# The Fourier branch of an encoder block, computed in halves: even and odd in token and channel

## The chip, the cores and the metric

The kernel runs on one core of a Trainium2 chip. A core has a matrix engine (TensorE, PE in the profile; PEld is its loading of stationary tiles), a vector engine (VectorE, DVE), a scalar engine (ScalarE, ACT), a general one (GpSimd, POOL) and a sync engine (SP) from which most transfers from memory are issued. Each engine has a queue of its own and works it off in order; semaphores tie the queues together. The metric is the device time of one execution in microseconds (us); for several runs, their median.

## The reference

One encoder block for 256 tokens (SEQ) of 2048 channels (D_MODEL), in float32. Two token mixers work side by side on the normalised input: a gated DeltaNet with 8 heads of 128 and a Fourier branch with 8 groups of 128 channels. Their outputs are gated channel by channel, added and projected, and a squared-ReLU MLP follows. Cut to what matters here:

```python
h = rms_norm(x, g_mix[l])
q, k, v, z, f, scal, gates = jnp.split(h @ w_in[l], SPLIT_POINTS, axis=-1)
y_a = gated_deltanet_branch(q, k, v, z, scal, ...)     # ends with  ... @ w_dn_up
y_f = fourier_branch(f, w_fourier[l])
gate_a, gate_f = jnp.split(jax.nn.sigmoid(gates), N_BRANCHES, axis=-1)
x = x + (gate_a * y_a + gate_f * y_f) @ w_o[l]

def fourier_branch(f, w_lin):
    fg = f.astype(jnp.float32).reshape(b, t, N_FOURIER_GROUPS, FOURIER_GROUP_DIM)
    fr = jnp.real(jnp.fft.fft2(fg, axes=(1, 3), norm="ortho"))
    return fr.reshape(b, t, FOURIER_WIDTH).astype(f.dtype) @ w_lin
```

For each group the real part of the two-dimensional transform over tokens and channels is C_T f C_D - S_T f S_D, with cosine and sine tables. Cosine is even and sine odd under the reflection of a token t to 256 - t and of a channel d to 128 - d.

## The kernel before

Every product is made in split precision: each operand is cut into a high part and a low part (type fp32r), and high times high, high times low and low times high are added up, three matmuls for one. Activations are cut once. Weights are cut on the fly. A weight tile of 128 x 1024 floats (512 KB) is loaded by SP into one of four buffers named `raw`; `split` makes its high part `hi` on ACT (L88) and its low part `lo` on DVE (L92), three buffers each; TensorE then uses them. `wtiles` hands out the buffers. Two routines use them around the change:

- `stream(src, nk, ahi, alo)` holds the activations stationary (128 tokens of one k tile, for two token halves tb) and moves weights of 512 columns: 6 matmuls for each k (L167 to L169). A chunk of 512 outputs with 16 k tiles is 96 matmuls and 8 weight tiles; with 8 k tiles it is half of that.
- `split` also cuts results that go into the next product, such as `o_hi` and `o_lo`.

The program around the change, in order:

- `dn_group(0)` and `dn_group(1)`: the DeltaNet. Its buffers are in the pool `pd`. Its last part, `dn_out`, forms the heads' outputs `ohat` (L602), their norms and, on POOL, the factors `fsc` (L614). Matmuls of the following gates fill its pauses on TensorE.
- `gates` 0 to 3: four chunks of the DeltaNet gate, `stream` over `w_g` and a tanh on ACT into the columns of `merged`.
- the head norm: `ohat` times `fsc` and `zs` (L671), four transposes for each group and token half (L675), split into `o_hi` and `o_lo`.
- w_dn: `stream` over `w_dn` in four chunks with `o_hi` and `o_lo`; the gate is multiplied in. Then the pool `pd` is closed.
- the f projection: `stream` over the last two chunks of `w_in`, 1024 Fourier channels. `f1`, `fe`: sum and difference of the two token halves (t and t + 128), split into `f_hi`, `f_lo`.
- the DFT: eight groups, each with 6 matmuls along tokens (L722 to L727) and 6 along channels (L736), 256 columns each, then a split into `fr_hi`, `fr_lo`.
- `gates_f` 0 to 3, chunks 4 to 7 of the gates, and after each (one chunk ahead) `merge`: `stream` over `w_fo` with `fr_hi`, `fr_lo`, gate and sum (L752, L753), transposes (L756), split into `m_hi`, `m_lo`.
- `xres` and `gfin`, loaded on ACT's queue into memory that the merge's pool `pf` leaves; then w_o, `stream` over four chunks with `m_hi`, `m_lo`, and the MLP.

The program is written in this order, but a scheduler that works on the whole program places each instruction in its engine's queue, so that queues can differ from the code's order where no dependence forbids it. Pools are memory: a tile that takes the place of another waits until that one's last user is done.

## Time and profile before

| | us |
|---|---|
| median of three runs | 1401.39 (1400.87 to 1401.4) |
| the profiled execution | 1398.59 |
| its span in the trace | 1396.9 |
| TensorE busy in it | 1381.9 |
| VectorE busy in it | 864.6 |
| ScalarE busy in it | 689.5 |
| one low part of a weight tile on VectorE | 1.224 |
| one high part of a weight tile on ScalarE | 1.060 |

The span is the time from the first to the last instruction that the profiler recorded in one execution; durations below are from that execution. Busy time of TensorE is modelled from the starts of pipelined matmuls: the mean duration that a row gives for one matmul is longer than the distance from one start to the next. A row of the timeline gives start and duration in us, the engine, the line, the operation, output and inputs, shapes and count; a row of the groups gives the count, the busy us, the mean ns of one and the idle time of the engine just before. A row of the windows gives a stretch of the span, the busy time and count of each engine in it, the granted clock of TensorE as a share of full speed, the busy share of the transfer engines and GB/s.

### The profile page before, as it was taken

To read this page: it belongs to the slowest core of one execution; us is meant where nothing else is said; L and a number is where in the kernel's file an instruction comes from. 1 tells how busy PE (TensorE), PEld (TensorE's weight loads), DVE (VectorE), ACT (ScalarE), POOL (GpSimd) and SP (SyncE) were. 2 spreads that over 40 slices of the span, in tenths; PEclk is the share of its full clock that TensorE was granted. 3 is DMA by queue.
4 is the path that set the end of the run, shared out by engine and by line. 5 is a ranking of instruction groups with operands and counts; after the bars stand their busy time and mean duration, and the time that the engine had idled before them with its cause. 6 is when DMAs were issued, how large, how long until landed. Compare 5 with 4: busy or idle time off the path is not lost.

```text
span 1396.9 us, 20162 instructions
## 1 busy us (share of the span) xinstructions
PE 1381.9 (99%) x7838; PEld 1195.6 (86%) x7838; DVE 864.6 (62%) x1239; ACT 689.5 (49%) x1042; POOL 35.8 (3%) x60
## 2 busy tenths in 40 slices
PE   9999999999999999999999999999999999999997
PEld 8999997888888888888888888888888888888897
DVE  7869997845556555656666665444456666644553
ACT  6586746545435444445545544333344544444443
POOL 2001100101000000000000000000000000000000
PEclk9999999999999999999999999999999999999999
DMA  8556466354566556676555556666655555666663
GB/s 286 151 169 176 157 162 175 104 151 136 184 204 180 152 181 187 210 251 183 183 192 185 189 185 189 192 194 194 196 188 188 186 191 183 187 193 194 194 195 122
DMA packets 94544, 255.63 MB, mean 183 GB/s; under 512 B 25456, under 2 KB 33648, under 8 KB 94064
## 3 DMA queue, kind: packets, MB, share of 16 engines
q1 hardware_dynamic: 93456, 250.15, 58.4%
q10 hardware_dynamic: 992, 4.19, 0.8%
q8 instruction: 61, 1.00, 0.3%
q14 instruction: 35, 0.29, 0.1%
HBM read 251.16 MB, written 3.15 MB: 182 GB/s over the span
## 4 chain that ended last, share of the span: by engine, by line
PE 95%; issue 1%; DVE 1%; DMA 1%; ACT 1%; SPq 0%; POOLq 0%; POOL 0%; DVEq 0%; ACTq 0%
PE mm L146 17%; PE mm L167 10%; PE mm L168 10%; PE mm L169 10%; PE mm L145 8%; PE mm L829 8%; PE mm L827 8%; PE mm L828 8%; PE mm L122 3%; PE mm L121 3%; PE mm L127 3%; PE mm L148 1%; DMA raw<-in_w_k_dram 0%; PE aux L736 0%; DVE lo L92 0%
## 5 line engine op out<-in xcount | busy, mean ns | idle before, releaser
L92 DVE TENSOR_TENSOR lo<-raw,hi 128x1024 fp32r<-128x1024 f32 (+1 forms) x459 | 560.3, 1221 | 396.1 <-ACT hi L88 390.7
L88 ACT ACTIVATE hi<-raw 128x1024 fp32r<-128x1024 f32 (+1 forms) x459 | 485.6, 1058 | 475.9 <-PE mm L829 185.8
L146 PE MATMUL mm<-hh,hi 128*128 128x512 f32 x1024 | 356.8, 398 | 0.0
L145 PE MATMUL mm<-hh,lo 128*128 128x256 f32 x960 | 269.3, 281 | 0.0
L146 PEld LDWEIGHTS mm<-hh,hi 128*128 128x128 f32 x1024 | 188.1, 188 | 41.6
L828 PE MATMUL mm<-lo,rh 128*128 128x512 f32 (+1 forms) x512 | 192.3, 376 | 0.0
L829 PE MATMUL mm<-hi,rl 128*128 128x512 f32 (+1 forms) x512 | 192.3, 376 | 0.0
L145 PEld LDWEIGHTS mm<-hh,lo 128*128 128x128 f32 x960 | 181.5, 189 | 2.9
L827 PE MATMUL mm<-hi,rh 128*128 128x512 f32 (+1 forms) x512 | 173.7, 376 | 0.0
L168 PE MATMUL mm<-lo,hh 128*128 128x512 f32 x384 | 151.6, 395 | 0.0
L169 PE MATMUL mm<-hi,hh 128*128 128x512 f32 x384 | 150.9, 393 | 0.0
L167 PE MATMUL mm<-hi,hh 128*128 128x512 f32 x384 | 143.2, 394 | 0.4 <-ACT merged L653 0.4
L828 PEld LDWEIGHTS mm<-lo,rh 128*128 128x128 f32 x512 | 96.4, 188 | 17.6
L829 PEld LDWEIGHTS mm<-hi,rl 128*128 128x128 f32 x512 | 96.4, 188 | 17.4
L827 PEld LDWEIGHTS mm<-hi,rh 128*128 128x128 f32 x512 | 96.3, 188 | 17.3
L122 PE MATMUL mm<-hh,hi 128*128 128x256 f32 x320 | 90.6, 283 | 0.0
L121 PE MATMUL mm<-hh,hi 128*128 128x256 f32 x320 | 90.5, 283 | 0.0
L127 PE MATMUL mm<-hh,lo 128*128 128x256 f32 x320 | 90.4, 283 | 0.0
L167 PEld LDWEIGHTS mm<-hi,hh 128*128 128x128 f32 x384 | 72.3, 189 | 15.5 <-ACT merged L653 0.6
L168 PEld LDWEIGHTS mm<-lo,hh 128*128 128x128 f32 x384 | 72.5, 189 | 14.3
L169 PEld LDWEIGHTS mm<-hi,hh 128*128 128x128 f32 x384 | 72.6, 189 | 14.0
L152 ACT COPY rt<-mm 128x256 f32<-128x256 f32 x64 | 23.9, 373 | 109.1 <-PE mm L146 109.1
(312 smaller groups left out, 1654.1 us busy)
## 6 DMA issues: line engine op xcount, KB each, us to landing
raw<-in_w_up_dram SPq DMA_DIRECT2D x128, 512.0 KB, 3.7
raw<-in_w_down_dram SPq DMA_DIRECT2D x128, 512.0 KB, 3.5
raw<-in_w_g_dram SPq DMA_DIRECT2D x64, 512.0 KB, 3.8
raw<-in_w_qkv_dram SPq DMA_DIRECT2D x40, 512.0 KB, 4.3
raw<-in_w_in_dram SPq DMA_DIRECT2D x32, 512.0 KB, 3.9
raw<-in_w_o_dram SPq DMA_DIRECT2D x32, 512.0 KB, 4.3
raw<-in_w_dn_dram SPq DMA_DIRECT2D x16, 512.0 KB, 3.6
raw<-in_w_fo_dram SPq DMA_DIRECT2D x16, 512.0 KB, 3.5
```

The lines of the kernel that those rows point to most:

```text
L88: act.activation(hi, src, AF.Copy, scale=scale)
L92: dve.tensor_tensor(lo, src2, hi.bitcast(F32), op=ALU.subtract)
L121: first = pe.matmul(o, hv[:, cs], ahi[:, k, :], start=(k == 0), stop=False)
L122: pe.matmul(o, hv[:, cs], alo[:, k, :], start=False, stop=False)
L145: pe.matmul(ps[:, 0:T], lv[:, cs], ab[:, k, 0], start=False, stop=False)
L146: pe.matmul(ps, hv[:, cs], ab[:, k].rearrange("p a b -> p (a b)"), start=(k == 0), stop=(k == KD - 1))
L167: pe.matmul(ps[tb], ah, hi[:, kk, :], start=(k == 0), stop=False)
L168: pe.matmul(ps[tb], ah, lo[:, kk, :], start=False, stop=False)
L169: pe.matmul(ps[tb], al, hi[:, kk, :], start=False, stop=(k == nk - 1))
L827: pe.matmul(ps[tb], ah, hi[:, kk, :], start=(k == 0), stop=False)
L828: pe.matmul(ps[tb], ah, lo[:, kk, :], start=False, stop=False)
L829: pe.matmul(ps[tb], al_, hi[:, kk, :], start=False, stop=(k == 31))
```

## The change

The Fourier branch now uses the reflections. Instead of f, the sums and differences of reflected tokens (`ev`: t plus 256 - t, 129 columns padded to 130; `od`: t minus 256 - t, 128 columns) are multiplied with the sums and differences of the weights of reflected channels (d plus 128 - d, and d minus 128 - d). Each pair of 512 KB weight tiles `w_fa`, `w_fb` (channels below 64, and their reflections) is added and subtracted on chip by `halves`, and each result is split like any weight tile. The same is done with `w_fourier` on the output side, in `y_f`. Channel 64 of each group, which is its own reflection, goes apart: `f_last` and the small tables `w_fon`, `dfn`. The tokens are loaded a second time from `xT` and normalised and folded by `fold`. Weights are now stationary and tokens move: `mm2` multiplies a high part with both parts of the tokens (256 or 260 columns) and a low part with the high part (128 or 130 columns), two matmuls where there were three. `f_pair(j)`, for two groups each, gives the even and the odd half of f; `transform` does the DFT on the halves and is placed after the second w_dn chunk; `y_f(n)`, for two times 128 output channels, multiplies with the folded `w_fourier`, joins the halves and leaves channels on the partitions, so that the gates are transposed instead of the result (`channels`).

The order of the stages changes: f_pair and f_last now come ahead of w_dn. The pool `pd` is closed right after the DeltaNet; what lives longer (`ohat`, `zs`, `fsc`, `o_hi`, `o_lo`) moves to a new pool `pk`. The arithmetic of the tables and the reordering of the weights into tiles happen in the preparation of the inputs, with no sums of weights there.

The diff, cut to its core:

```diff
@@ dn_group(1, "q") @@
+    dnp.close()
...
+    def mm2(o, hi, lo, ab, n, start, stop):
+        first = None
+        if not start:
+            first = pe.matmul(o[:, 0:n], lo, ab[:, 0], start=False, stop=False)
+        last = pe.matmul(o, hi, ab.rearrange("p a b -> p (a b)"), start=start, stop=stop)
+        if start:
+            first = last
+            pe.matmul(o[:, 0:n], lo, ab[:, 0], start=False, stop=False)
+        return first, last
...
+    ev = pm.tile([P, KD, 2, E0], F32R, tag="sC", name="ev")
+    od = pm.tile([P, KD, 2, P], F32R, tag="sD", name="od")
+    def fold(c):
+        ks = slice(4 * c, 4 * c + 4)
+        x4 = pq.tile([P, 4, T], F32, tag="x4", bufs=2, name=nm("x4"))
+        nc.sync.dma_start(x4, xT[:, ks, :])
+        for k in range(4):
+            act.activation(x4[:, k, :], x4[:, k, :], AF.Copy, scale=gm[:, 4 * c + k:4 * c + k + 1])
+        dve.tensor_tensor(x4, x4, rbc.unsqueeze(1).to_broadcast([P, 4, T]), op=ALU.mult)
+        e4 = pq.tile([P, 4, E0], F32, tag="e4", bufs=1, name=nm("e4"))
+        o4 = pq.tile([P, 4, P], F32, tag="o4", bufs=1, name=nm("o4"))
+        act.copy(e4[:, :, 0:E0:P], x4[:, :, 0:E0:P])
+        act.activation(e4[:, :, E0 - 1:E0], x4[:, :, 0:1], AF.Copy, scale=0.0)
+        act.activation(o4[:, :, 0:1], x4[:, :, 0:1], AF.Copy, scale=0.0)
+        dve.tensor_tensor(e4[:, :, 1:P], x4[:, :, 1:P], x4[:, :, T - 1:P:-1], op=ALU.add)
+        dve.tensor_tensor(o4[:, :, 1:P], x4[:, :, 1:P], x4[:, :, T - 1:P:-1], op=ALU.subtract)
+        split(ev[:, ks, 0, :], ev[:, ks, 1, :], e4)
+        split(od[:, ks, 0, :], od[:, ks, 1, :], o4)
+    def halves(a_src, b_src):
+        ra, _, _ = wtiles(parts=False)
+        rb, _, _ = wtiles(parts=False)
+        nc.sync.dma_start(ra.rearrange("p a b -> p (a b)"), a_src)
+        nc.sync.dma_start(rb.rearrange("p a b -> p (a b)"), b_src)
+        rp = pf.tile([P, KP, NW], F32, tag="rp", bufs=2, name=nm("rp"))
+        _, ph, pl = wtiles(raw=False)
+        dve.tensor_tensor(rp, ra, rb, op=ALU.add)
+        split(ph, pl, rp)
+        _, mh, ml = wtiles(raw=False)
+        dve.tensor_tensor(ra, ra, rb, op=ALU.subtract)
+        split(mh, ml, ra)
+        return [tuple(x.rearrange("p a b -> p (a b)") for x in t) for t in ((ph, pl), (mh, ml))]
+    def sum_halves(dst, ps, n):
+        act.copy(dst, ps[:, n:2 * n])
+        dve.tensor_tensor(dst, ps[:, 0:n], dst, op=ALU.add)
...
+    def f_pair(j):
+        pp, pq_ = mm_ps()[:, 0:2 * E0], mm_ps()[:, 0:2 * P]
+        for q in range(2):
+            wp, wm = halves(w_fa[j, :, q * 1024:q * 1024 + 1024], w_fb[j, :, q * 1024:q * 1024 + 1024])
+            for (o, w, ab, n) in ((pp, wp, ev, E0), (pq_, wm, od, P)):
+                for kk in range(8):
+                    k = 8 * q + kk
+                    cs = slice(kk * P, kk * P + P)
+                    mm2(o, w[0][:, cs], w[1][:, cs], ab[:, k], n, k == 0, k == KD - 1)
+        es = pf.tile([P, E0], F32, tag="es", bufs=1, name=nm("es"))
+        os_ = pf.tile([P, P], F32, tag="os", bufs=1, name=nm("os"))
+        sum_halves(es, pp, E0)
+        split(Ph[:, j], Pl[:, j], es)
+        sum_halves(os_, pq_, P)
+        split(Qh[:, j], Ql[:, j], os_)
+    def f_last():
+        raw, hi, lo = wtiles(1, P)
+        nc.sync.dma_start(raw[:, 0], w_fn)
+        split(hi, lo, raw)
+        ps = mm_ps()[0:8, 0:2 * E0]
+        for k in range(KD):
+            cs = slice(8 * k, 8 * k + 8)
+            mm2(ps, hi[:, 0, cs], lo[:, 0, cs], ev[:, k], E0, k == 0, k == KD - 1)
+        es = pf.tile([8, E0], F32, tag="es", bufs=1, name=nm("es"))
+        sum_halves(es, ps, E0)
+        split(P8h, P8l, es)
...
+    def y_f(n):
+        wp, wm = halves(w_fo[n // 2, 0], w_fo[n // 2, 1])
+        raw = pt_.tile([8, 256], F32, tag="w8", bufs=1, name=nm("w8"))
+        nc.sync.dma_start(raw, w_fon[:, n * P:n * P + 256])
+        w8 = tuple(pt_.tile([8, 256], F32R, tag=f"w8{i}", bufs=1, name=nm("w8")) for i in range(2))
+        split(w8[0], w8[1], raw)
+        e = pt_.tile([P, 2, E0], F32, tag="ee", bufs=1, name=nm("ee"))
+        oc = pt_.tile([P, 2, P], F32, tag="oc", bufs=1, name=nm("oc"))
+        pod = dn_ps()
+        last = None
+        for i in range(2):
+            o = mm_ps()[:, 0:2 * E0]
+            for j in range(4):
+                cs = slice(i * NW + j * P, i * NW + j * P + P)
+                mm2(o, wp[0][:, cs], wp[1][:, cs], fe[:, j], E0, j == 0, False)
+            mm2(o, w8[0][:, i * P:i * P + P], w8[1][:, i * P:i * P + P], f8, E0, False, True)
+            sum_halves(e[:, i], o, E0)
+        for i in range(2):
+            o = pod[:, i * T:i * T + T]
+            for j in range(4):
+                cs = slice(i * NW + j * P, i * NW + j * P + P)
+                first, end = mm2(o, wm[0][:, cs], wm[1][:, cs], fo[:, j], P, j == 0, j == 3)
+                if j == 0:
+                    after(first, last)
+            last = end
+        pv = pod.rearrange("p (i a b) -> p i a b", i=2, a=2)
+        act.copy(oc, pv[:, :, 1])
+        dve.tensor_tensor(oc, pv[:, :, 0], oc, op=ALU.add)
+        y = pt_.tile([P, 2, T], F32, tag="yf", bufs=2, name=nm("yf"))
+        act.copy(y[:, :, P:P + 1], e[:, :, P:P + 1])
+        dve.tensor_tensor(y[:, :, 0:P], e[:, :, 0:P], oc, op=ALU.add)
+        dve.tensor_tensor(y[:, :, P + 1:T], e[:, :, P - 1:0:-1], oc[:, :, P - 1:0:-1], op=ALU.subtract)
+        return y
...
+    with tc.tile_pool(name="pq", bufs=1) as pq:
+        for c in range(4):
+            gates(m_cols(c), c)
+            fold(c)
+            if c < 2:
+                head_norm(c)
+    dd, dn8 = table(dft, P, 2 * E0 + 256, "d"), table(dfn, 8, 5 * E0, "d8")
+    CD, SD = cut(dd, 0, E0), cut(dd, E0, P)
+    CT, ST = cut(dd, E0 + P, E0), cut(dd, 2 * E0 + P, P)
+    CD64 = [cut(dn8, j * E0, E0, 8) for j in range(4)]
+    CT128 = cut(dn8, 4 * E0, E0, 2)
+    for j in range(4):
+        f_pair(j)
+    f_last()
+    fctx2 = ExitStack()
+    for c in range(4):
+        ps = stream(w_dn[c], NH, o_hi, o_lo)
+        for tb, m in enumerate(m_cols(c)):
+            dve.scalar_tensor_tensor(m, m, 1.0, ps[tb], op0=ALU.add, op1=ALU.mult)
+        if c == 1:
+            transform()
+    fctx2.close()
...
-    f_hi = pf.tile([P, 2, 1024], F32R, tag="f_hi", name="f_hi")
-    f_lo = pf.tile([P, 2, 1024], F32R, tag="f_lo", name="f_lo")
-    for c in range(2):
-        ps = stream(w_in[2 + c], KD, h_hi, h_lo)
...
-    for gr in range(8):
...
     tg = gates_f(0)
     for c in range(4):
         nxt = gates_f(c + 1) if c < 3 else None
-        merge(c, tg)
+        for i in range(2):
+            n = 4 * c + 2 * i
+            y = y_f(n)
+            dve.scalar_tensor_tensor(y, channels(tg, 2 * P * i), 1.0, y, op0=ALU.add, op1=ALU.mult)
+            dve.tensor_tensor(y, channels(merged, n * P), y, op=ALU.add)
+            split(m_hi[:, n:n + 2, :], m_lo[:, n:n + 2, :], y)
         tg = nxt
```

`transform`, left out here, makes 102 such products of tables: 72 with stationary tiles of 128 columns and 30 with 2 or 8, all with 128 or 130 moving columns.

What this does to the queues is seen at three places. The first is DVE's queue where the last gate's weights are split, around the head norm. Before (L671 is the head norm's product, L602 the DeltaNet's last outputs, lo_3999 and its followers are low parts of w_dn tiles):

```order
L92 TENSOR_TENSOR lo_3912<-raw_3910,hi_3911 128x1024
L92 TENSOR_TENSOR lo_3930<-raw_3928,hi_3929 128x1024
L671 SCALAR_TENSOR_TENSOR ohat_3247<-ohat_3247,fsc,zs_3054 128x128 x4
L602 SCALAR_TENSOR_TENSOR ohat_3247<-dn_3335,eab,tmp_3250 128x128 x4
L94 SCALAR_TENSOR_TENSOR o_lo<-aux_3955,gh,o_hi 128x4x128
L94 SCALAR_TENSOR_TENSOR o_lo<-aux_3966,gh,o_hi 128x4x128
L92 TENSOR_TENSOR lo_3999<-raw_3997,hi_3998 128x1024
L671 SCALAR_TENSOR_TENSOR ohat_3247<-ohat_3247,fsc,zs_3054 128x128 x4
L92 TENSOR_TENSOR lo_4017<-raw_4015,hi_4016 128x1024
L92 TENSOR_TENSOR lo_4035<-raw_4033,hi_4034 128x1024
```

After (L882 is the head norm's product; L735 and L738 are the sum and the difference of two weight tiles, `rp` and `raw`; L716 the tokens times `rbc`; L722 and L723 the even and odd sums of tokens; `dl` and `d8l` low parts of tables):

```order
L882 SCALAR_TENSOR_TENSOR ohat_3250<-ohat_3250,fsc,zs_3057 128x128 x4
L735 TENSOR_TENSOR rp_4112<-raw_4108,raw_4109 128x1024
L92 TENSOR_TENSOR dl<-raw_4094,dh 128x516
L92 TENSOR_TENSOR d8l<-raw_4100,d8h 8x650
L738 TENSOR_TENSOR raw_4108<-raw_4108,raw_4109 128x1024
L92 TENSOR_TENSOR lo_4114<-rp_4112,hi_4113 128x1024
L716 TENSOR_TENSOR x_423_3529<-x_423_3529,rbc 128x1024
L735 TENSOR_TENSOR rp_4159<-raw_4155,raw_4156 128x1024
L722 TENSOR_TENSOR e_424_3536<-x_423_3529 128x4x127
L723 TENSOR_TENSOR o_425_3537<-x_423_3529 128x4x127
L716 TENSOR_TENSOR x_456_3719<-x_456_3719,rbc 128x1024
L738 TENSOR_TENSOR raw_4155<-raw_4155,raw_4156 128x1024
```

and a few rows on, up to what the first matmul of f_pair needs (`ev`):

```order
L94 SCALAR_TENSOR_TENSOR o_lo_3756<-aux_3741,gh,o_hi_3755 128x4x128
L94 SCALAR_TENSOR_TENSOR o_lo_3756<-aux_3750,gh,o_hi_3755 128x4x128
L92 TENSOR_TENSOR lo_4119<-raw_4108,hi_4118 128x1024
L92 TENSOR_TENSOR lo_4161<-rp_4159,hi_4160 128x1024
L92 TENSOR_TENSOR ev<-e_424_3536,ev 128x4x130
L92 TENSOR_TENSOR od<-o_425_3537,od 128x4x128
```

The low parts of w_dn's tiles, which stood right behind the head norm, have given their place to the folding of tokens and weights.

The second is TensorE's queue at the end of the last gate chunk (mm_3800 and mm_3801 before, mm_3927 and mm_3928 after). Before, transposes of `ohat` and w_dn follow:

```order
L168 MATMUL mm_3801<-lo_3930,hh 128x512
L169 MATMUL mm_3801<-hi_3929,hh 128x512
L675 MATMUL aux_3977<-tr,ohat_3247 128x128 x4
L167 MATMUL mm_3995<-hi_3998,o_hi 128x512
L167 MATMUL mm_3996<-hi_3998,o_hi 128x512
L168 MATMUL mm_3995<-lo_3999,o_hi 128x512
L169 MATMUL mm_3995<-hi_3998,o_lo 128x512
```

After, f_pair's first half follows, with ev and then od:

```order
L171 MATMUL mm_3928<-lo_4057,hh 128x512
L172 MATMUL mm_3928<-hi_4056,hh 128x512
L886 MATMUL aux_3750<-tr,ohat_3250 128x128 x4
L687 MATMUL mm_4106<-ev,hi_4113 128x260
L690 MATMUL mm_4106<-ev,lo_4114 128x130
L686 MATMUL mm_4106<-ev,lo_4114 128x130
...
L687 MATMUL mm_4106<-ev,hi_4113 128x260
L687 MATMUL mm_4107<-od,hi_4118 128x256
L690 MATMUL mm_4107<-od,lo_4119 128x128
L686 MATMUL mm_4107<-od,lo_4119 128x128
```

The matmuls of w_dn now stand behind all of f_pair and f_last.

The third is SP's queue behind the last tile of the gates:

```order
L163 DMA raw_4055<-in_w_g_dram 128x1024
L696 DMA raw_4094<-in_dft_dram 128x516
L696 DMA raw_4100<-in_dfn_dram 8x650
L731 DMA raw_4108<-in_w_fa_dram 128x1024
L732 DMA raw_4109<-in_w_fb_dram 128x1024
L713 DMA x_423_3529<-in_xT_dram 128x1024
L713 DMA x_456_3719<-in_xT_dram 128x1024
L731 DMA raw_4155<-in_w_fa_dram 128x1024
L732 DMA raw_4156<-in_w_fb_dram 128x1024
L731 DMA raw_4214<-in_w_fa_dram 128x1024
L713 DMA x_489_3909<-in_xT_dram 128x1024
```

Before, w_dn's tiles followed at this place; now two tables, the pairs of folded weights and the second load of the tokens do, in turn.

More of the change, by code (lines that the diff above doesn't have):

```diff
@@ L336, in encoder_block_kernel @@
     ohat = []
-    fsc = pd.tile([P, 2, 2, 4], F32, tag="fsc", name="fsc")
+    fsc = pk.tile([P, 2, 2, 4], F32, tag="fsc", name="fsc")
     De = pd.tile([P, 16, P], F32, tag="De", name="De")
@@ L668, in encoder_block_kernel, with head_norm @@
+    o_hi, o_lo = [], []
+    def head_norm(gi):
+        pts = []
         for tb in range(2):
```

229 lines of the change are left out of this document (143 added, 86 removed).

## The prediction

> **What bounds the kernel now.** First the page: how busy each engine is, and which engine the chain that ended last runs through.
>
> ```profile
> span 1396.9 us, 20162 instructions
> PE 1381.9 (99%) x7838; PEld 1195.6 (86%) x7838; DVE 864.6 (62%) x1239; ACT 689.5 (49%) x1042; POOL 35.8 (3%) x60
> ...
> PE 95%; issue 1%; DVE 1%; DMA 1%; ACT 1%; SPq 0%; POOLq 0%; POOL 0%; DVEq 0%; ACTq 0%
> ```
>
> TensorE (PE) is busy 99% of the span and makes 95% of the chain. Over the whole kernel VectorE (DVE) has 38% to spare, so a change that takes work from TensorE and gives it to DVE looks good from here. But a share over the span is an average. What counts is the stretch that changes: from the last weights that the merged gate needs to the start of the output projection. The timeline of TensorE gives its ends.
>
> ```profile
> 343.88 0.47 PE L169 MATMUL mm<-hi,hh 128*128 128x512 f32 x1
> ...
> 350.81 0.39 PE L169 MATMUL mm<-hi,hh 128*128 128x512 f32 x1
> 351.04 0.60 PE L675 MATMUL aux<-tr,ohat 128*128 128x128 f32 x4
> 351.39 0.70 PE L167 MATMUL mm<-hi,o_hi 128*128 128x512 f32 x2
> ...
> 585.26 0.62 PE L167 MATMUL mm<-hi,m_hi 128*128 128x512 f32 x2
> ```
>
> The last DeltaNet output matmul has been issued at 343.88 (gate matmuls go on), the gates end at 351.39, w_dn follows, and w_o begins at 585.26. Both programs hold the same instructions on TensorE before 343.88 and, but for 12 transposes, after the start of w_o. The windows view over these ends (busy time of PE, PEld, DVE, ACT, POOL, then granted clock, DMA share, GB/s):
>
> ```profile
> 343.88:351.39 7.51, 7.51 (x38) 6.21 (x37) 6.03 (x13) 5.14 (x14) 1.94 (x4) 1.00 0.40 131
> 351.39:396.70 45.31, 45.31 (x200) 36.53 (x199) 24.79 (x25) 18.65 (x19) 0.00 (x0) 1.00 0.59 185
> 396.70:585.26 188.56, 188.56 (x889) 158.03 (x888) 104.44 (x110) 86.88 (x101) 0.00 (x0) 1.00 0.60 181
> 343.88:585.26 241.38, 241.38 (x1122) 200.77 (x1121) 135.26 (x147) 110.68 (x133) 1.94 (x4) 1.00 0.59 180
> ```
>
> TensorE never pauses in these 241.38 us, at full clock. DVE works 135.26 us in them (56%), so the stretch lasts as long as its matmuls.
>
> **What a matmul costs.** The busy column gives a matmul's latency, and matmuls overlap; their cost is the distance from start to start. The w_dn window holds 192 matmuls of 512 columns and 8 transposes (0.9 us): 44.4/192 = 0.231. From 343.88 to 351.04 are 31 of them, 0.231 each; inside longer runs it is 0.227, which I use. For 128 and 256 columns:
>
> ```profile
> 341.28 0.39 PE L591 MATMUL dn<-Y,E 128*128 128x128 f32 x2
> ...
> 343.07 1.06 PE L599 MATMUL dn<-sF,offk 128*128 128x128 f32 x8
> ...
> 229.80 0.28 PE L367 MATMUL aux<-q,k 128*128 128x256 f32 x1
> 229.92 0.28 PE L371 MATMUL aux<-q,k 128*128 128x256 f32 x1
> 230.04 0.28 PE L372 MATMUL aux<-q,k 128*128 128x256 f32 x1
> ```
>
> The 24 passes of 128 columns from 341.28 to 343.88 step by 0.108, those of 256 by 0.12. Split-precision matmuls (fp32r) of 128 or 130 columns, which the change brings, occur nowhere in this trace. Bounds: from 512 to 256 columns the step falls by 0.107, or 0.42 ns a column, so 130 columns would be 0.067 if columns alone counted; the plain-f32 128-column products (L591) leave two records of 0.11 for one product, so 0.22 is the top. I take 0.110: each matmul brings a weight load of its own (7838 of both), and the single pass of 128 columns, the nearest row, is hardly shorter than that of 256, as if something other than its columns set it. For stationary tiles of 2 or 8 columns I take 0.067.
>
> The Trainium skill, page "TensorE: Matmul & The Clock Gate", section "Back-to-back issue gap", gives about 81 ns for a sustained matmul of 128 columns and 131 for 512. The rows here have 108 and 227, so the measurement decides; by the page's 81 the narrow matmuls of the transform and of four y_f would be 72 × 2 × 0.029 = 4 us cheaper, and the result 1420.
>
> **What TensorE loses and gains.** Gone: the f projection (2 chunks, 192 × 0.227 = 43.6), the DFT (96 × 0.118 = 11.3), the w_fo product (192 × 0.227 = 43.6) and 32 transposes (3.5): 102.0 us. New: four f_pair of 64 matmuls, half of 256/260 columns and half of 128/130 (128 × 0.121 + 128 × 0.110 in all, 29.6 for 256); f_last 16 × (0.121 + 0.067) = 3.0; transform 72 × 0.110 + 30 × 0.067 = 9.9; eight y_f of 18 × 0.120 + 18 × 0.110 = 4.15, 33.2; 64 transposes 7.0: 82.7 us. So **TensorE's work falls by 19.3 us**; were it still the bound, that would be the gain.
>
> **What DVE gains.** Durations by form:
>
> ```profile
> L92 DVE TENSOR_TENSOR lo<-raw,hi 128x1024 fp32r<-128x1024 f32 x457 | 559.0, 1224 | 396.1 <-ACT hi L88 390.7
> L753 DVE TENSOR_TENSOR merged<-merged,tg 128x512 f32<-128x512 f32 x8 | 5.1, 682 | 0.0
> L94 DVE SCALAR_TENSOR_TENSOR o_lo<-aux,gh,o_hi 128x512 fp32r<-128x512 f32 x4 | 2.8, 744 | 0.0
> L92 DVE TENSOR_TENSOR fr_lo<-aux,fr_hi 128x256 fp32r<-128x256 f32 x8 | 3.4, 426 | 7.0 <-ACT fr_hi L88 7.0
> L489 DVE TENSOR_TENSOR Xf<-Xf,tf 128x128 f32<-128x128 f32 x2 | 0.6, 292 | 0.1
> L88 ACT ACTIVATE hi<-raw 128x1024 fp32r<-128x1024 f32 x457 | 484.3, 1060 | 475.8 <-PE mm L829 185.8 <-PE mm L169 167.1 <-PE mm L146 69.3
> L194 ACT ACTIVATE hh<-xts,gm 128x256 fp32r<-128x256 f32 x14 | 6.1, 500 | 1.4 <-DMA xts<-in_xT_dram 1.4
> ```
>
> A weight tile costs DVE one pass of 1.224 today. `halves` takes two tiles, adds, subtracts and then splits both results: four passes of 1.224, twice as much per tile, for matmuls worth less: 32 per pair (16 × 0.121 + 16 × 0.110 = 3.7 us of TensorE against 4.9 of DVE). In today's stream two tiles are 24 × 0.227 = 5.4 of TensorE against 2.4 of DVE.
>
> *The f phase.* When may it start? The folding stands under the gates in the code, but in DVE's queue all of it comes behind the last head-norm product (L671 before, L882 after). Its memory is that of DeltaNet's pool, closed just before, and SP's first x load waits for the last reader there, POOL's fsc.
>
> ```profile
> 347.91 0.54 POOL L614 TENSOR_TENSOR fsc<-ov,rq 128x4 f32<-128x4 f32 x1
> ...
> 348.48 1.14 DVE L671 SCALAR_TENSOR_TENSOR ohat<-ohat,fsc,zs 128x128 f32<-128x128 f32 x4
> ```
>
> So DVE starts at 349.6 with: 8 halves × 4 passes and 4 products with rbc, 36 × 1.224 = 44.1; 16 passes of about 512 elements (even and odd sums, their low parts) × 0.682 = 10.9; the tables' low parts (516 and 650 columns) 1.5; o_lo twice 0.744 = 1.5; 12 small ones (sums and splits of P and Q) × 0.30 = 3.6. That is 61.6, to 411.2. For the loads I add 1.3: they land 3.5 to 3.8 us after issue,
>
> ```profile
> raw<-in_w_g_dram SPq DMA_DIRECT2D x64, 512.0 KB, 3.8
> ```
>
> and with two of the four raw buffers per half the first ones come late. So the last low part is ready at 412.5; its 16 matmuls take 1.85 and f_last 3.0: **417.4**. TensorE's gates end at 351.4; from there it takes 66.0 us for 32.6 us of matmuls. About 33 us are idle: some 14 at the start (the first matmul waits for the low part of `ev`, the sixteenth row of DVE's queue, 16 us of work), the rest between the halves. ACT does not bind: per half two passes of 1.060, and 16 scalings of x at 0.500. Nothing covers the wait, since in TensorE's queue f_pair stands ahead of w_dn, whose matmuls need none of it.
>
> *The rest.* w_dn 44.4 as now, with the transform's 9.9 (its small splits lie beside w_dn's matmuls) and gates_f 384 × 0.227 = 87.2. Eight y_f 33.2, and 48 of the transposes 5.2. Two y_f follow each of gates_f(1) and (2), whose 21.8 us of matmuls let DVE get ahead; four follow gates_f(3) with nothing between. There DVE needs per y_f: 4 × 1.224 + 2 × 0.682 for the gate products, one low part 0.682, sums and small passes 2.3 (two of 0.292, four of 0.426), in all 9.3 against 4.6 of TensorE. Of this excess some is worked off ahead; from the end of gates_f(3) to w_o I get 24.8 instead of 17.9: 6.9 of stall. 16 transposes instead of 4 fall into w_o (12 × 0.109 = 1.3), and w_o's residual, loaded when the merge's memory is free, may come 0.5 late.
>
> *Sum.* 7.5 (gates) + 66.0 + 44.4 + 9.9 + 87.2 + 33.2 + 5.2 + 6.9 = 260.3, against 241.4: +18.9; with 1.3 and 0.5, +20.7. A last term is the clock:
>
> ```profile
> 220.00:225.00 5.00, 4.82 (x75) 3.92 (x76) 3.65 (x4) 4.85 (x15) 0.00 (x0) 0.76 0.54 80
> ...
> 222.83 0.63 PE L168 MATMUL mm<-lo,hh 128*128 128x512 f32 x1
> 223.26 0.63 PE L169 MATMUL mm<-hi,hh 128*128 128x512 f32 x1
> ...
> 226.13 0.40 PE L169 MATMUL mm<-hi,hh 128*128 128x512 f32 x1
> 226.36 0.39 PE L168 MATMUL mm<-lo,hh 128*128 128x512 f32 x1
> ```
>
> Where TensorE had little to do, just before, its clock fell to 0.76 over 5 us and the same matmul stepped by 0.43 instead of 0.23, for about 3 us: 1.5 us lost. In the f phase DVE hides that; once, where w_dn or w_o begins, I count it: +22.2. The profiled execution took 1398.59 us (span 1396.9), so 1420.8; the median of the runs, 1401.39, is 2.8 above it: **1424**.
>
> **The rivals.**
> *TensorE stays the bound* (0.07). Then the 19.3 us are saved: 1382. It decides at 3.7 us of DVE per half; the four passes alone need 4.9, so they would have to be a quarter cheaper and the folding to lie under the gates. For it: DVE's 38% of slack. Against it: the queue order, and 61.6 against 32.6.
> *Both cancel* (0.05): the folding runs early (15 us of the idle time go) and y_f's stall is hidden: 1424 − 15 − 7 = 1402. Against it speaks that x waits for fsc at 348.45.
> *Narrow matmuls at the price of plain f32* (0.2): 0.22 for each of 130 or 128 columns. The f phase hides its own but for the last 8 and f_last (0.9 + 2.4); transform 102 × 0.22 − 9.9 = 12.5; the four y_f that TensorE bounds 4 × 18 × 0.11 = 7.9; the other four stay within DVE's 9.3. Together 23.7: 1448. At the lower bound of 0.067, −7: 1417.
> *The clock stays low* (0.12): TensorE pauses in every half of the f phase, and at half clock a half costs it 7.4 us, more than the 5.8 that DVE takes from 366 to 412; eight of them and a slow f_last (6) end at about 431, +14: 1438. The trace shows one such dip and its recovery in 3 us of work; a TensorE that becomes the bound would be busy and recover, which speaks against it. The Trainium skill, same page, section "Part 1: The HAM clock gate (the "warmup" mystery)", says that the clock halves after an idle window of about 3.4 us and comes back after as long a busy one; the 0.43 beside 0.23 agrees, and by that rule the clock drops at least once in the first 14 us of waiting.
>
> **How the numbers follow.** The forecast, with its own range of 1414 to 1431 (narrow matmuls at 0.067, loads that cost each half up to 1 us more), has 0.56. The range for all, 1412 to 1450, takes in the narrow matmuls and the low clock and leaves out the rivals below, 0.12, and tails. A measurement of this kernel tells 0.2% (2.8 us) from no change: faster 0.07, same 0.05, slower 0.88.
>
> **What would show it.** After: TensorE idle from about 351 to 366, its releaser DVE's `ev` or `lo`; DVE near 100% busy from 350 to 412 and f_last's end near 417; DVE's `halves` passes at 1.22 each; the transform's matmuls stepping by 0.11; gates_f without a pause, then four y_f in some 9 us each, TensorE half idle; w_o beginning near 606. I would be wrong if DVE's adds cost clearly less than 1.2, if TensorE found matmuls to run ahead of the f phase, or if narrow matmuls step by 0.2.

## The result and the profile after

The changed kernel takes 1437.93 us (median of four runs, 1435.25 to 1443.18) against 1401.39 us before: ratio 1.0266, 95% interval 1.0235 to 1.0296, 36.5 us slower. The execution that was profiled is the slowest of the four, 1443.18 us; its mean granted clock is 0.979, that of the other three 0.984 to 0.985, so its stages hold more time at a lower clock than those of the median run. Its page, span and engines first and then the chain of waits:

```profile
span 1441.4 us, 20881 instructions
PE 1401.3 (97%) x8068; PEld 1207.8 (84%) x8068; DVE 923.9 (64%) x1348; ACT 708.6 (49%) x1129; POOL 35.5 (2%) x60
...
PE 68%; DVE 3%; DMA 2%; issue 1%; ACT 1%; POOL 0%; POOLq 0%; DVEq 0%; ACTq 0%
```

TensorE had been 95% of the chain and is 68% now (the page's shares do not add up to 100 here); VectorE and the loads have come in. VectorE's busy time grew by 59 us. The windows view of the changed kernel by stage (busy time of PE, PEld, DVE, ACT, POOL, then granted clock, DMA share, GB/s): the rest of the gates, the f phase, w_dn with the transform, the gates_f stages with the first four y_f, and the last four y_f.

```profile
349.21:357.57 8.36, 8.28 (x42) 6.51 (x40) 5.45 (x13) 4.51 (x14) 1.60 (x4) 1.00 0.55 190
357.57:422.89 65.32, 43.81 (x295) 40.69 (x295) 56.38 (x72) 35.32 (x73) 0.00 (x0) 0.74 0.50 164
422.89:482.42 59.53, 59.53 (x290) 47.04 (x289) 28.53 (x40) 21.37 (x32) 0.00 (x0) 0.97 0.47 149
482.42:593.38 110.96, 110.96 (x569) 93.17 (x568) 77.17 (x91) 53.17 (x72) 0.00 (x0) 1.00 0.61 190
593.38:618.59 25.21, 24.68 (x157) 22.77 (x156) 22.55 (x34) 12.84 (x26) 0.00 (x0) 0.80 0.57 172
349.21:618.59 269.38, 247.25 (x1348) 210.18 (x1347) 190.08 (x245) 127.21 (x213) 1.60 (x4) 0.91 0.55 173
```

The f phase takes 65.3 us, 21.5 of them without a matmul, while VectorE works 56.4. In the last four y_f VectorE works 22.6 of 25.2 us, and TensorE counts as busy for 24.7 of them at a granted clock of 0.80. The stretch that took 241.4 us takes 269.4. The timeline of TensorE shows the wait at the head of the f phase, and slow matmuls behind it:

```profile
356.89 0.60 PE L886 MATMUL aux<-tr,ohat 128*128 128x128 f32 x4
370.98 0.56 PE L687 MATMUL mm<-ev,hi 128*128 128x260 f32 x1 [13.49 <-issue]
...
371.66 0.53 PE L687 MATMUL mm<-ev,hi 128*128 128x260 f32 x1
371.98 0.31 PE L686 MATMUL mm<-ev,lo 128*128 128x130 f32 x1
372.09 0.53 PE L687 MATMUL mm<-ev,hi 128*128 128x260 f32 x1
...
396.96 0.33 PE L687 MATMUL mm<-ev,hi 128*128 128x260 f32 x1
397.13 0.22 PE L686 MATMUL mm<-ev,lo 128*128 128x130 f32 x1
397.19 0.34 PE L687 MATMUL mm<-ev,hi 128*128 128x260 f32 x1
```

A pair of a wide and a narrow matmul takes 0.43 us at 371 and 0.23 at 397. The windows view shows when the granted clock fell: within the first 2.5 us of the wait, some 11 us before the first matmul of f_pair, and it is still 0.50 over the first 23 us of f_pair:

```profile
357.57:360.00 2.43, 0.00 (x0) 0.00 (x0) 2.43 (x3) 2.43 (x7) 0.00 (x0) 0.98 0.93 263
360.00:371.00 11.00, 0.02 (x1) 0.05 (x1) 9.39 (x12) 7.41 (x18) 0.00 (x0) 0.50 0.55 194
371.00:394.00 23.00, 17.73 (x74) 16.27 (x75) 19.24 (x24) 9.62 (x23) 0.00 (x0) 0.50 0.33 107
```

The kernel also lost time where nothing was changed. From the start of w_o to the end of the span it takes 1441.4 - 618.59 = 822.8 us; before it was 1396.9 - 585.26 = 811.6. So 11.2 of the 44.6 us between the two profiled executions lie in a part with the same instructions in the same order, but for 12 transposes. A window of 100 us inside the down projection, before and then after:

```profile
900.00:1000.00 100.00, 100.00 (x443) 82.84 (x442) 48.76 (x43) 39.20 (x37) 0.00 (x0) 1.00 0.66 194
```

```profile
938.00:1038.00 100.00, 100.00 (x430) 80.56 (x429) 47.30 (x43) 38.16 (x36) 0.00 (x0) 1.00 0.63 186
```

TensorE does not pause and the granted clock is 1.00 in both, but 443 matmuls are done in one and 430 in the other: 0.226 against 0.233 us each. The last piece, 5.3 us, stands ahead of the stretch (343.88 before, 349.21 after, for the same end of the DeltaNet); it varies from run to run, 343.7 to 348.0 in the profiled executions of the variants below. The median run is also 5.3 us below the profiled one, but which of its stages are shorter no trace shows.

### The profile page after: what moved, and what is told of

The parts are those of the page before. It is cut to its first block, busy times and chain, and to the rows that moved or that the text cites. A ratio compares the mean times of both kernels' runs of the same rounds, so it can differ in the third digit from the quotient of the medians.

```text
span 1441.4 us, 20881 instructions
## 1 busy us (share of the span) xinstructions
PE 1401.3 (97%) x8068; PEld 1207.8 (84%) x8068; DVE 923.9 (64%) x1348; ACT 708.6 (49%) x1129; POOL 35.5 (2%) x60
## 4 chain that ended last, share of the span: by engine, by line
PE 68%; DVE 3%; DMA 2%; issue 1%; ACT 1%; POOL 0%; POOLq 0%; DVEq 0%; ACTq 0%
PE mm L146 17%; PE mm L145 8%; PE mm L1011 8%; PE mm L1010 8%; PE mm L1012 8%; PE mm L171 5%; PE mm L172 5%; PE mm L170 5%; PE mm L687 1%; DVE lo L92 1%; DMA raw<-in_w_fb_dram 1%; DVE rp L735 1%; DVE raw L738 1%; DMA raw<-in_w_fo_dram 1%; PE dn L687 1%
## 5 line engine op out<-in xcount | busy, mean ns | idle before, releaser
L92 DVE TENSOR_TENSOR lo<-raw,hi 128x1024 fp32r<-128x1024 f32 (+2 forms) x444 | 540.6, 1219 | 363.6 <-ACT hi L88 357.5
L88 ACT ACTIVATE hi<-raw 128x1024 fp32r<-128x1024 f32 (+2 forms) x444 | 468.7, 1056 | 460.3 <-PE mm L1012 194.7
L1011 PE MATMUL mm<-lo,rh 128*128 128x512 f32 (+1 forms) x512 | 195.6, 382 | 0.0
L171 PE MATMUL mm<-lo,hh 128*128 128x512 f32 x320 | 127.9, 400 | 0.0
L172 PE MATMUL mm<-hi,hh 128*128 128x512 f32 x320 | 126.4, 395 | 0.0
L170 PE MATMUL mm<-hi,hh 128*128 128x512 f32 x320 | 118.5, 395 | 1.1 <-ACT hi L88 0.7
L170 PEld LDWEIGHTS mm<-hi,hh 128*128 128x128 f32 x320 | 59.7, 189 | 13.8 <-ACT hi L88 1.2
L171 PEld LDWEIGHTS mm<-lo,hh 128*128 128x128 f32 x320 | 60.7, 190 | 12.4
L172 PEld LDWEIGHTS mm<-hi,hh 128*128 128x128 f32 x320 | 60.7, 190 | 12.0
```

What stands on the lines that cost most here:

```text
L88: act.activation(hi, src, AF.Copy, scale=scale)
L92: dve.tensor_tensor(lo, src2, hi.bitcast(F32), op=ALU.subtract)
L170: pe.matmul(ps[tb], ah, hi[:, kk, :], start=(k == 0), stop=False)
L171: pe.matmul(ps[tb], ah, lo[:, kk, :], start=False, stop=False)
L172: pe.matmul(ps[tb], al, hi[:, kk, :], start=False, stop=(k == nk - 1))
L1011: pe.matmul(ps[tb], ah, lo[:, kk, :], start=False, stop=False)
```

## The experiments

**A shift of 64 bytes (e1, e2, e4).** What differs for the down projection is where its stationary tiles lie. The new pool `pk` begins with `fsc`, 64 bytes a partition, and `ev` is 256 bytes longer than the tile `m_hi` whose place it takes; so m_hi, m_lo, rh and rl lie 64 or 320 bytes (modulo 1024) further from the weight tiles than before.

e1, the kernel before:

```diff
+    padp = ctx.enter_context(tc.tile_pool(name="padp", bufs=1))
+    pad = padp.tile([P, 16], F32, tag="pad", name="pad")
+    pool.memset(pad, 0.0)
     pm = ctx.enter_context(tc.tile_pool(name="pm", bufs=1))
```

> The kernel before with one tile of 64 bytes a partition ahead of the pool pm; every queue keeps its order, and m_hi, m_lo, rh and rl lie 64 bytes further on, as the new 64-byte tile fsc puts them in the changed kernel. Theory A (the address of the stationary tile sets the step of a matmul of 512 columns): the 384 matmuls of w_o and the 1344 of the down projection step by 0.231 to 0.236 us instead of 0.227, about 1728 x 0.0065 = +11 us, 1412 us; the gates stay at 0.227. Rival B (the longer steps of the changed kernel come from its run or its traffic): 0.227 throughout, within 2 us of 1401.4.

Measured: 1414.41 us against 1401.2, ratio 1.0090 (1.0075 to 1.0105). The same window:

```profile
900.00:1000.00 100.00, 100.00 (x430) 80.60 (x429) 48.13 (x42) 37.41 (x36) 0.00 (x0) 1.00 0.58 189
```

430 matmuls, as in the changed kernel. A tile of 64 bytes that is never read costs 13 us.

e2, the changed kernel:

```diff
+    pad = pm.tile([P, 240], F32, tag="pad", name="pad")
+    pool.memset(pad[:, 0:16], 0.0)
-    ev = pm.tile([P, KD, 2, E0], F32R, tag="sC", name="ev")
+    ev = pm.tile([P, 4352], F32R, tag="sC", name="ev")[:, 0:KD * 2 * E0].rearrange("p (a b c) -> p a b c", a=KD, b=2)
...
-            r = po.tile([P, T], F32, tag="rr", bufs=4, name=nm("rr"))
+            i = rri[0] % 4
+            rri[0] += 1
+            r = (po if i == 3 else pk).tile([P, T], F32, tag=("ohat1", "zs0", "zs1", "rr")[i], bufs=1, name=nm("rr"))
```

> The changed kernel with 960 bytes of padding ahead of ev and 768 behind it, so that m_hi, m_lo, rh and rl lie at the same place within 1024 bytes as before; the room comes from the tiles rr, three of which move to the pool pk. Every queue keeps its order. Theory A: w_o and the down projection step by 0.227 again, 10 to 11 us less, about 1427 us. Rival B: 0.231 to 0.236 as in the changed kernel, about 1438.

Measured: 1425.77 us, 12.2 less than the changed kernel, ratio to before 1.0182 (1.0158 to 1.0206). The window holds 443 again:

```profile
900.00:1000.00 100.00, 100.00 (x443) 82.84 (x442) 47.35 (x42) 39.26 (x37) 0.00 (x0) 1.00 0.59 192
```

e4, the kernel before with every tile from the weight buffers on 352 bytes further:

```diff
-    ones = cp.tile([P, P], F32, name="ones")
+    ones = cp.tile([P, P + 88], F32, name="ones")[:, 0:P]
```

> The kernel before with 352 unused bytes in the first pool, so that all weight tiles and stationary tiles lie 352 bytes further on, all at multiples of 1024, at the same distances from each other; every queue keeps its order. Theory A1 (the distance between the moving and the stationary tile counts): 0.227 as before, within 2 us of 1401.4. Theory A2 (the address by itself counts): the step of 512 columns changes everywhere, by -0.007 to +0.009 us for about 3000 matmuls, so by 10 to 27 us in one direction.

Measured: 1399.09 us, ratio 0.9984 (0.9975 to 0.9994); 443 matmuls in the window.

```profile
900.00:1000.00 100.00, 100.00 (x443) 82.84 (x442) 49.31 (x43) 38.62 (x38) 0.00 (x0) 1.00 0.60 194
```

Moved together by 352 bytes the tiles keep their step; with the stationary tile alone moved by 64 they lose 3%. From the start of w_o to the end of the span the profiled executions take 822.2 us in e1 and 812.5 in e2, beside 822.8 in the changed kernel and 811.6 before: that is where the 11.2 us come from. So where the stationary tile lies sets the step, and e4 speaks for its distance from the moving tile. That its address by itself does not count is not shown: the tiles were moved together by 352 bytes, never by the 64 that cost the time. A rule for all distances is not known from this. About a third of the change's loss, 12 of 36 us, is this, and has nothing to do with the Fourier branch.

**VectorE's passes taken away (e3).** e3, the changed kernel without the folding of the weights:

```diff
-        rp = pf.tile([P, KP, NW], F32, tag="rp", bufs=2, name=nm("rp"))
-        dve.tensor_tensor(rp, ra, rb, op=ALU.add)
-        split(ph, pl, rp)
+        split(ph, pl, ra)
-        dve.tensor_tensor(ra, ra, rb, op=ALU.subtract)
-        split(mh, ml, ra)
+        split(mh, ml, rb)
```

> The changed kernel without the sum and the difference in halves: the two weight tiles are split as they are (this leaves the folding of the weights out). VectorE has two passes less for each of 16 halves. Theory (VectorE's passes set the f phase and the last four y_f): the f phase, from the end of the gates to the first w_dn matmul, falls from 65 us by 16 x 1.22 = 20 us to about 45, TensorE's 33 us and the wait for the first ev still showing; the run of four y_f falls from 25 to about 20; in all 22 to 27 us less, about 1413. Rival (the loads set it: half of a half's time is the wait for w_fb): the f phase stays above 58 us, less than 8 us gained.

Measured: 1422.27 us, 15.7 less than the changed kernel; a gain, but short of 22. The edit takes two things away at once, 16 passes and VectorE's wait for `w_fb`, since no pass needs both tiles any more. The f phase and its two parts behind the first wait:

```profile
354.30:407.70 53.40, 42.50 (x301) 40.17 (x299) 39.15 (x56) 34.96 (x73) 0.00 (x0) 0.78 0.61 209
363.70:380.00 16.30, 14.48 (x59) 13.17 (x60) 12.44 (x17) 9.65 (x25) 0.00 (x0) 0.50 0.42 132
380.00:407.70 27.70, 27.23 (x237) 26.54 (x237) 19.21 (x30) 17.21 (x30) 0.00 (x0) 0.97 0.67 225
```

The phase fell from 65.3 to 53.4, by 12 and not by 20. With VectorE out of the way TensorE is the next limit: 14.5 of 16.3 us busy at a clock of 0.50, then 27.2 of 27.7 at 0.97. The half clock would account for the 8 us that are missing (half of 16.3); e3 was not run with the clock kept up. The rival, that the loads set the phase, falls: with the same loads 53.4 is under its 58, and it gained more than 8.

**The clock kept up (e6).** The changed kernel, realigned (e2), with 60 idle products where TensorE waits:

```diff
+            if gi == 1 and tb == 1:
+                for _ in range(60):
+                    pe.matmul(wps[:, 0:P], oh[:, 3, :], ident, start=True, stop=True)
```

> The realigned changed kernel (e2) with 60 idle products of 128 columns (13 us) in TensorE's queue between the last head-norm transposes and the first matmul of f_pair, where it waits; the result does not use them. Theory V (VectorE and the loads set the f phase, the low clock is hidden): the granted clock at the start of f_pair is 1.0 instead of 0.5, and the f phase is at most 3 us shorter: 1423 to 1427. Rival C (the half clock in the first 23 us of f_pair costs): the f phase is 6 to 10 us shorter, 1416 to 1420.

Measured: 1429.76 us, not below e2's 1425.77. (The two profiled executions are 6.2 us apart; 4.0 of them lie ahead of the stretch, in the DeltaNet.) The f phase of e2, and then of e6 the f phase, the idle products in it, and what follows them:

```profile
351.40:418.10 66.70, 44.45 (x299) 41.08 (x298) 56.85 (x72) 36.06 (x74) 0.00 (x0) 0.74 0.48 162
```

```profile
355.40:424.70 69.30, 55.91 (x421) 52.74 (x420) 57.45 (x73) 35.85 (x75) 0.00 (x0) 0.88 0.47 157
355.40:369.40 14.00, 14.00 (x126) 13.87 (x125) 12.16 (x14) 9.77 (x25) 0.00 (x0) 1.00 0.64 217
369.40:390.00 20.60, 13.55 (x69) 11.99 (x67) 17.80 (x22) 10.21 (x21) 0.00 (x0) 0.67 0.34 116
```

The clock holds 1.00 through the products and then falls again, to a mean of 0.67, because TensorE waits between the halves; the phase is no shorter (69.3 against 66.7). Rival C, 6 to 10 us less, finds no support. The test is a weak one, though: the clock stood at 0.50 for 23 us of f_pair's work in e2 and still for 17 in e6, and a clock held up through the whole phase was not tried. What speaks for VectorE being later anyway is the row of 371 to 394 above: even at half clock TensorE is without a matmul for 5.3 of the 23 us.

**The same work in another order (e5).** If VectorE's four passes per half cost because nothing covers them, other matmuls beside them must bring the time back. e5 is e2 with w_dn first and the folding under it, and then halves and weight tiles of gates_f in turn; the core of the edit:

```diff
+C1 = (1, 1, 1, 1, 1, 1, 2, 2)
+D1, D2 = 2, 2
+E1 = (3, 3, 2, 2, 2, 2, 2, 2)
...
+    S = gates_g()
+    for j in range(4):
+        H = f_pair(j)
+        go(H)
+        go(S, C1[2 * j])
+        go(H)
+        go(S, C1[2 * j + 1])
+    f_last()
+    go(S, D1)
+    transform()
+    go(S, D2)
...
+    for u in range(8):
+        pend.append((u, y_f(2 * u)))
+        go(S, E1[u])
```

`gates_g` goes on by one weight tile of gates_f at each step, f_pair by one half.

> The realigned changed kernel (e2) with its stages written in another order: w_dn comes first, with the folding of the tokens under it; then each half of f_pair alternates with one or two weight tiles of gates_f; four tiles of gates_f stand around the transform, and each y_f alternates with two or three. Nothing else is changed; the four gate tiles take the place of o_hi, o_lo, ohat and zs. Theory (the time was lost because four passes of VectorE per half had no other matmuls beside them): over the f phase and the gates VectorE then needs 56 us for 57 us of matmuls, over the y_f phase 99 for 93; TensorE is busy nearly throughout, its work is 19 us less than before, and the stretch from the end of DeltaNet to w_o falls from 265 us (e2) to about 228, against 241 before: 1386 to 1396. Rival (the loads or the three buffers of hi and lo hold it up, or VectorE's passes show all the same): TensorE still idle by 20 us or more, 1405 to 1420.

Measured: 1404.36 us, 21.4 less than e2, ratio to before 1.0018 (1.0008 to 1.0027). It ended between the two, at the rival's edge, but the rival's sign, 20 us of idle TensorE, did not show. The stretch took 244.1 us instead of 265, and TensorE worked 236.5 of them:

```profile
400.00:475.00 75.00, 68.53 (x438) 59.80 (x437) 54.09 (x63) 34.74 (x49) 0.00 (x0) 0.98 0.60 195
475.00:507.00 32.00, 31.48 (x183) 25.50 (x181) 16.50 (x25) 13.08 (x23) 0.00 (x0) 0.95 0.37 124
507.00:589.90 82.90, 82.90 (x496) 71.53 (x495) 73.81 (x108) 44.71 (x78) 0.00 (x0) 1.00 0.57 182
345.80:589.90 244.10, 236.54 (x1344) 199.31 (x1343) 190.81 (x253) 127.91 (x217) 2.05 (x5) 0.99 0.57 189
```

The idle time came from VectorE's queue, its passes and its waits for `w_fb`, standing uncovered; covering takes most of it away, and does not tell the two apart. What is left in the f phase (the first row) are 6.5 us in which TensorE waits for a low part, though VectorE is busy only 54 of 75 us.

**The subtraction on GpSimd (e7, e8, e9).** One line in `halves`, in e5 (e7) and in e2 (e8):

```diff
-        dve.tensor_tensor(ra, ra, rb, op=ALU.subtract)
+        pool.tensor_tensor(ra, ra, rb, op=ALU.subtract)
```

> The interleaved kernel (e5) with the subtraction of halves on GpSimd instead of VectorE, 16 passes of 128 x 1024. e5 still lost some 9 us in the f phase to low parts that came late and 3 to 5 us in the y_f phase. Theory (these waits are VectorE's passes): with 16 x 1.22 = 20 us off VectorE they go, 8 to 12 us less: 1392 to 1398, faster than before. Rival (GpSimd's pass is so slow, or slows VectorE's passes by sharing its way to the memory, that the waits move to it): 1402 to 1412; the mean of a VectorE low part would then be above 1.3 us or GpSimd's pass above 5.

> The realigned changed kernel (e2, 1425.8) in its own order, with the subtraction of halves on GpSimd. Theory (VectorE's passes set the f phase and the last four y_f): 8 x 1.22 = 10 us less in the f phase, 4 x 1.22 = 5 in the y_f run, less what the low clock and the loads then take (e3 kept two thirds): 1412 to 1418. Rival (GpSimd's pass stands in the chain of each half and is longer than the one it replaces): no gain or a loss, 1424 to 1435.

Measured: e7 1408.38 us, 4.0 more than e5; e8 1437.94, 12.2 more than e2. e7 lies in its rival's range, e8 3 us above its rival's. Groups of e8, GpSimd's pass and the low parts of the sums, and the latter in e2:

```profile
L740 POOL TENSOR_TENSOR raw<-raw,raw 128x1024 f32<-128x1024 f32 x16 | 47.4, 2962 | 213.2 <-DVE rp L737 205.0 <-DMA raw<-in_w_fa_dram 5.8 <-ACT hi L88 2.4
L92 DVE TENSOR_TENSOR lo<-rp,hi 128x1024 fp32r<-128x1024 f32 x16 | 24.3, 1518 | 8.8 <-ACT hi L88 8.7
```

```profile
L92 DVE TENSOR_TENSOR lo<-rp,hi 128x1024 fp32r<-128x1024 f32 x16 | 19.5, 1217 | 3.6 <-ACT hi L88 3.6
```

GpSimd needs 2.96 us for what took VectorE 1.22, and VectorE's low parts of the sums beside it go from 1.22 to 1.52 on average. The Trainium skill, page "SBUF — State Buffer", section "Who interferes with whom", says that a VectorE instruction with two inputs in that memory contends with a GpSimd instruction that reads it; 1217 against 1518 ns agrees.

e9 is e7 with e4's 352 bytes.

> e7 with the 352 unused bytes of e4 in the first pool, so that the weight tiles and m, rh, rl start at multiples of 1024. e4 was 2 us faster than before, at steps of 0.227 that had not changed. If that belongs to the addresses it shows again, 2 us below e7; if it was a chip's or a run's, within 1 us of e7.

Measured: 1406.01 us (1404.04 to 1410.48) against e7's 1408.38 (1404.93 to 1411.72): the ranges overlap, nothing is settled by it.

**A fourth buffer (e10, e11), and a wider transform (e12).** e10, from e5:

```diff
-        _, ph, pl = wtiles(raw=False)
+        ph = pf.tile([P, KP, NW], F32R, tag="ph", name=nm("ph"))
+        pl = pf.tile([P, KP, NW], F32R, tag="pl", name=nm("pl"))
```

> The interleaved kernel (e5) with a high-part and a low-part buffer of their own for the sums of halves, so that a half and a weight tile of gates_f share four of each instead of three (and 608 bytes of padding, so that the new buffers lie at the same place within 1024 bytes as hi). Theory (e5's 9 us of waits for low parts in the f phase came from full buffers: VectorE was busy only 47 of 62 us there): they fall to some 3 us, and the y_f phase gains 1 or 2: 1395 to 1399, faster than before by 0.2 to 0.4%. Rival (the waits are VectorE's order: the low part wanted stands behind other passes): no change, 1402 to 1406.

Measured: 1401.41 us, ratio to before 0.9996 (0.9988 to 1.0004): 3 us less than e5 and no difference to before. The f phase, the transform, and the whole stretch:

```profile
401.60:465.00 63.40, 61.17 (x415) 54.77 (x414) 51.09 (x59) 30.59 (x44) 0.00 (x0) 1.00 0.69 220
465.00:505.00 40.00, 39.48 (x205) 31.78 (x204) 18.91 (x28) 15.21 (x27) 0.00 (x0) 0.87 0.43 132
...
347.50:587.90 240.40, 237.46 (x1345) 200.05 (x1344) 191.32 (x253) 126.44 (x217) 2.10 (x6) 0.98 0.60 192
```

The waits of the f phase fell from 6.5 to 2.2 us: full buffers had made most of them, as the theory said. The next place is the transform, where TensorE counts as busy and its clock is 0.87 over 40 us.

> e10 with the 352 unused bytes of e4 in the first pool. If the 2 us that e4 and e9 showed belong to the addresses, 2 us below e10; otherwise within 1 us of it.

Measured (e10 with e4's 352 bytes): 1400.7 us, 1.0000 of before (0.9991 to 1.0009), 0.7 below e10. The 2 us of e4 did not come again clearly; what they were stays open.

e12 is e10 with other counts:

```diff
-C1 = (1, 1, 1, 1, 1, 1, 2, 2)
-D1, D2 = 2, 2
-E1 = (3, 3, 2, 2, 2, 2, 2, 2)
+C1 = (1, 1, 1, 1, 1, 1, 1, 1)
+D1, D2 = 4, 6
+E1 = (2, 2, 2, 2, 2, 2, 1, 1)
```

> e10 with ten instead of four weight tiles of gates_f around the transform (one with each half of f_pair, ten around the transform, the rest one or two with each y_f). In e10 the granted clock fell to 0.87 over the 40 us of the transform, 5 us, with 3 us of waits at its end. Theory (the transform's many narrow matmuls in a row leave TensorE so little to do that its clock drops; between long matmuls it would stay up): the clock stays above 0.95 there, 3 to 6 us less, 1395 to 1398. Rival (what the transform gains the y_f phase loses, which has four tiles fewer to cover VectorE): 1400 to 1405.

Measured: 1395.87 us (1392.41 to 1397.25), ratio to before **0.9962** (0.9949 to 0.9975). The transform and the stretch:

```profile
457.00:505.00 48.00, 48.00 (x249) 38.91 (x248) 24.39 (x32) 19.87 (x30) 0.00 (x0) 0.96 0.51 160
505.00:580.80 75.80, 75.80 (x474) 65.75 (x473) 69.50 (x104) 41.62 (x76) 0.00 (x0) 1.00 0.55 180
345.20:580.80 235.60, 234.33 (x1344) 197.57 (x1344) 189.54 (x251) 126.74 (x217) 2.10 (x6) 0.99 0.60 197
```

The clock is 0.96 there (over all runs the mean clock is 0.995 to 0.997, in e10 0.992 to 0.995), and the y_f phase, with fewer tiles to cover it, still shows no idle TensorE. The halves do pay, by 5.5 us, once their place and order are right: this version is faster than both kernels.

## Why the prediction was right, and where it was not

The sign and the mechanism, VectorE's queue without cover, were right; the size was short: 1424 forecast, 1437.93 measured, inside 1412 to 1450 but above the forecast's own 1414 to 1431. Term by term, in the profiled execution:

- **The f phase**, 66.0 forecast, 65.3 measured. VectorE's queue ran in the order that was counted, and its `halves` passes took 1.22 us each by their records:

```profile
L735 DVE TENSOR_TENSOR rp<-raw,raw 128x1024 f32<-128x1024 f32 x16 | 19.6, 1222 | 11.9 <-DMA raw<-in_w_fb_dram 6.8 <-DMA raw<-in_w_fo_dram 5.1
L738 DVE TENSOR_TENSOR raw<-raw,raw 128x1024 f32<-128x1024 f32 x16 | 19.5, 1217 | 0.2
```

  That the phase came out right is in part luck, since two terms were off by about as much in opposite directions. The waits for `w_fb` were 6.8 us where 1.3 were added. The passes were taken at their full duration, and they overlap a little:

```profile
371.29 1.22 DVE L735 TENSOR_TENSOR rp<-raw,raw 128x1024 f32<-128x1024 f32 x1
372.43 1.22 DVE L716 TENSOR_TENSOR x<-x,rbc 128x1024 f32<-128x1024 f32 x1
373.56 0.68 DVE L722 TENSOR_TENSOR e<-x 128x508 f32<-128x508 f32 x1
374.16 0.68 DVE L723 TENSOR_TENSOR o<-x 128x508 f32<-128x508 f32 x1
```

  From start to start they step by 1.13 and 0.60. From the first sum (354.31) to the end of the last low part (417.5) the durations of the 68 passes add up to 61 us, as forecast, but they occupy 56.3. e3 and e5 show that VectorE's queue without cover set this phase; its passes and its waits for `w_fb` were not separated, and the half clock was tested only in part (e6).
- **Narrow matmuls**, taken at 0.110: a pair of 260 and 130 columns steps by 0.23 at full clock, as 0.121 + 0.110 gave, though divided otherwise, 0.17 and 0.06. That they cost what plain f32 does is refuted.
- **w_dn and the transform**, 54.3 forecast, 59.5 measured. The clock, 0.97, is 1.8 of it. e2 has the same matmuls there at full clock and still takes 58.1:

```profile
418.12:476.18 58.06, 58.06 (x291) 45.84 (x289) 28.53 (x40) 21.46 (x32) 0.00 (x0) 1.00 0.45 152
```

  Summed from start to start in e2's trace, the transform takes 12.4 where 9.9 was written and w_dn's matmuls 46.1 where 44.4 was. Within the transform, matmuls of one form with 128 stationary columns mostly step by 0.11, as forecast; where the form changes the step is longer, 0.21 from 128 rows to 8 and 0.33 from a matmul of 512 columns to one of 8 rows.
- **gates_f and y_f**, 132.5 forecast (87.2 + 33.2 + 5.2 + 6.9), 136.2 measured; of this the last four y_f were 25.2 where 24.8 was written. That agreement is luck too. TensorE was to be half idle there, and it waits 0.5 us; 10.2 of the 25.2 us ran at half clock, which the sum does not have. e2, at full clock, takes 21.6 with TensorE busy for 20.4. First the changed kernel, then e2:

```profile
605.70:615.90 10.20, 10.20 (x46) 9.42 (x46) 9.66 (x19) 4.65 (x9) 0.00 (x0) 0.50 0.55 160
```

```profile
587.15:608.77 21.62, 20.36 (x157) 18.55 (x156) 20.44 (x32) 13.05 (x26) 0.00 (x0) 1.00 0.53 166
```

  So the 6.9 us of stall were little more than 1 in e2, and the y_f matmuls, 37.9 us in e2's trace where 33.2 was written, made up for most of the difference.
- **From w_o on**, 1.8 forecast (1.3 + 0.5), 11.2 measured. This is the step that failed: "Both programs hold the same instructions on TensorE before 343.88 and, but for 12 transposes, after the start of w_o" was taken to mean the same time. It did not look at where the tiles lie. e1 and e2 put 12 to 13 us on it; without it the changed kernel takes 1425.77, beside 1424.

The rival "the clock stays low" had its mechanism in part right (0.50 from 360 to 394), and that its 1438 is what was measured is chance: e2 reaches 1425.77 with the same low clock in the f phase. That VectorE hid it there, as the sum said, is likely but tested only in part (e6). The rival "TensorE stays the bound" was right in that TensorE can be made the bound again (e10, e12), and wrong in its 1382: of the 19.3 us of matmuls saved, e12 gets 241.4 - 235.6 = 5.8 in the stretch, with TensorE busy 234.3 of 235.6. So the new matmuls cost some 12 us more than the counts times the steps gave; that is a term mis-sized. Summed from start to start in e12's trace, y_f takes 38.7 us where 33.2 was written, the transform 12.5 for 9.9, f_pair 30.7 for 29.6, and the 414 matmuls of the gates in the stretch 98.6 where they would take 94.4 at the mean step before, 0.228; some 1.6 of the last is half clock.

## What to carry to other kernels

Work that is moved from a bound engine to an idle one is only free where it lies beside matmuls: count both engines in the stretch that changes, not over the span, and alternate stages with opposite needs in the order of the program. Compare the addresses of matmul operands between two versions: a small tile put in front of them can cost more than the change itself is worth. A lower granted clock is a loss only where TensorE is the one waited for.
